# Hybrid retention, gated linear attention and sliding-window block: GLA queries and keys move into the paired products, branch products become the heads' filling, moving sums and stores in another order

## The chip, the cores and the metric

The kernel runs on one core of a Trainium2 chip. The time is device microseconds of one launch, the median over several runs. PE is the tensor engine, DVE the vector engine, ACT the scalar engine, POOL GpSimd, SP the sync engine, which here only issues DMAs.

## The reference

One transformer block on 1024 tokens of width 1024, in float32. All matmuls are wanted at nearly float32 accuracy.

```python
h = rmsnorm(x, norm_mix_pre)
proj = h @ w_in
rq, rk, rv, rg, gq, gk, gv, gg, ga, sq, sk, sv, gate_logits = split(proj)
o_ret = head_groupnorm(retention(rq, rk, rv)) * silu(rg)          # 4 heads, dk 128, dv 256
log_a = max(log_sigmoid(ga @ alpha2 + b) / 16, -1)
o_gla = head_rmsnorm(gla(gq, gk, gv, log_a)) * silu(gg)           # 4 heads, chunks of 64 tokens
o_swa = swa_sinks(sq, sk, sv, sinks)                              # 16 query heads, window 128
projected = einsum('bsnc,ncd->bsnd', stack(o_ret, o_gla, o_swa), w_branch)
merged = sum(sigmoid(gate_logits) * projected, over the 3 branches)
x = x + rmsnorm(merged @ w_out, norm_mix_post)
h = rmsnorm(x, norm_ffn_pre)
f = (silu(h @ w_gate) * (h @ w_up)) @ w_down                      # width 2816
x = x + rmsnorm(f, norm_ffn_post)
```

In GLA, queries are multiplied by exp(b) and keys by exp(-b), b the running sum of log_a within a chunk; these factors lie in DRAM as `ed`.

## The kernel before

Each float32 operand is cut into a rounded high part (a cast on ACT, line 127) and a residue (a subtraction on DVE, line 128); a product is three matmuls, high x high, high x low, low x high. So PE works in groups of three, mostly 128x128 weights on 512 moving columns (token halves).

The program goes through these stages. *First phase* (up to about 100 us): x is normed, transposed on PE in two token halves (tiles `xps`, `hf`, the halves `hT`), first products and the window's values (`swa_values`, tile `sv`) run between. *Dense products*: feature-major columns of w_in go through `class Pairs`: two column blocks by two token halves form a 2x2 block product that is done with seven block products in place of eight (Strassen-Winograd): 84 matmuls for two blocks. `p1` to `p7` are the seven; the stationary sums s1 to s4 are made by `sums`/`split` from the weights, the moving sums t1 to t4 by `class Sums` from the normed input, made once. `steps` runs the first `lead` pairs together, so that each t is made and used once for all, then the rest in turn; results leave as held outputs (`held`) and snapshots `sn` in SBUF. *Window attention*, with token-major values v as filling (`lin_values`). *Heads*: eight recurrences (four of retention, four GLA, `i` from 0 to 7); each has short products with waits between, and takes filling from `lin_fill`: a generator that gives 12 matmuls per step. *Branches* (`branches`): 24 products of w_branch, 48 matmuls each, times the gate, summed over the branches into `mgd`. *Output rows* (`out_mm`, `out_norm`, eight rows, stores x1d), *feed-forward up* (pairs of gate and up columns, again with `Pairs`, lead 3, stores fT), *down* (`down_load`, `down_mm`, two token halves, stores out).

The GLA queries and keys go through `lin_qk`: plain products, 48 matmuls per column block, in `lin_stream` behind each head's values, as filling of the heads. The first partial sums of the branches stay in SBUF.

Tiles come from pools: 45 slots of 4 KB per partition (`dt_`), 18 of 2 KB (`bt`), eight PSUM banks. In the first part (line 76) the instructions of an engine stand in the order in which the code is written; from there on a scheduler sets the order per engine from its estimates. The queues are in order: a DMA that waits for a slot holds all that stand behind it on the same engine.

## Time and profile before

| | |
|---|---|
| median of 3 runs | 2200.08 us (2199.95 to 2202.84) |
| profiled execution | 2200.43 us |
| its span, first to last instruction | 2198.7 us |
| mean granted clock of PE | 0.983 |
| PE, DVE, ACT, POOL busy | 96%, 55%, 42%, 11% |

A busy share is an average over all stages. A matmul is shown with its whole passage, so neighbours overlap; the time from one start to the next is what counts. "[6.00 <-ACT s L127]" means that the engine was idle for 6.00 us and that the instruction that ended this is the one of ACT on line 127 that wrote tile s.

### The profile page before, as it was taken

What the parts mean: (1) busy time and instruction counts of PE and PEld (TensorE: products, weight loads), DVE (VectorE), ACT (ScalarE), POOL (GpSimd) and SP (SyncE); (2) the same over time, 40 slices, a digit from 0 to 9 for tenths busy, and PEclk for the clock granted to TensorE, in tenths of its full rate; (3) what the DMA queues carried; (4) which work ended last, traced back from release to release, by engine and by line L of the source; (5) the groups of instructions that cost most, each with busy time, mean ns of one, the idle gap of its engine ahead of it and who ended that gap; (6) DMA issues with size and microseconds to landing.
All of it is one profiled execution on the core that took longest, in us unless ns stands there. A gap on an engine that the chain in (4) does not pass through costs nothing. (4 is left out here: it accounts for less than half of the span.)

```text
span 2198.7 us, 28731 instructions
## 1 busy us (share of the span) xinstructions
PE 2114.9 (96%) x10660; PEld 1789.7 (81%) x10660; DVE 1205.9 (55%) x2219; ACT 914.1 (42%) x1772; POOL 240.9 (11%) x413
## 2 busy tenths in 40 slices
PE   6899999999999999999989999998999999999998
PEld 5678888888889989998967888876788888878786
DVE  4778754444438986555554444346565555544351
ACT  5455544444447774444342221255433333343240
POOL 3011000000012322332321000031000000000000
PEclk8999999999999999999989999999999999999999
DMA  5369655555565437656474542242454455473441
GB/s 186 108 215 271 211 168 172 161 161 159 179 221 179 150 132 268 239 190 228 149 263 138 173 144 96 96 134 77 132 146 136 138 144 144 125 267 140 169 176 39
DMA packets 343277, 364.06 MB, mean 166 GB/s; under 512 B 16464, under 2 KB 267728, under 8 KB 343136
## 3 DMA queue, kind: packets, MB, share of 16 engines
q1 hardware_dynamic: 299776, 265.20, 39.4%
q10 hardware_dynamic: 30816, 54.02, 6.7%
q0 software_dynamic: 12544, 43.00, 5.1%
q8 instruction: 84, 1.38, 0.3%
q14 instruction: 57, 0.47, 0.1%
HBM read 264.64 MB, written 97.52 MB: 165 GB/s over the span
## 5 line engine op out<-in xcount | busy, mean ns | idle before, releaser
L128 DVE TENSOR_TENSOR wl<-raw,wh 128x1024 fp32r<-128x1024 f32 x131 | 159.9, 1221 | 149.0 <-ACT wh L127 83.4
L127 ACT CAST s<-raw 128x512 fp32r<-128x512 f32 x200 | 120.6, 620 | 225.1 <-DVE raw L381 73.5
L127 ACT CAST wh<-raw 128x1024 fp32r<-128x1024 f32 x141 | 147.2, 1046 | 149.7 <-DMA raw<-in_w_down 58.9
L406 PE MATMUL x<-t,s 128*128 128x512 f32 x408 | 158.2, 392 | 5.7 <-ACT s L127 2.8
L407 PE MATMUL x<-t,s 128*128 128x512 f32 x408 | 159.7, 391 | 0.5 <-DVE t L128 0.3
L408 PE MATMUL x<-t,s 128*128 128x512 f32 x408 | 159.1, 390 | 0.0
L242 PE MATMUL pf<-o,wh 128*128 128x512 f32 x384 | 148.8, 394 | 8.4 <-ACT o L127 8.4
L243 PE MATMUL pf<-o,wh 128*128 128x512 f32 x384 | 149.7, 392 | 0.2 <-DVE o L128 0.2
L257 PE MATMUL v<-wh,hT 128*128 128x256 f32 x512 | 146.2, 285 | 0.0
L356 ACT COPY sn<-x 128x512 f32<-128x512 f32 x151 | 88.2, 585 | 137.3 <-PE x L408 131.0
L259 PE MATMUL v<-wh,hT 128*128 128x256 f32 x512 | 145.2, 284 | 0.0
L258 PE MATMUL v<-wl,hT 128*128 128x256 f32 x512 | 145.2, 284 | 0.0
L1334 PE MATMUL dn<-wh,f 128*128 128x512 f32 x352 | 137.0, 392 | 4.2 <-ACT f L127 4.2
L1335 PE MATMUL dn<-wl,f 128*128 128x512 f32 x352 | 136.9, 391 | 0.0
L128 DVE TENSOR_TENSOR s<-raw,s 128x512 fp32r<-128x512 f32 x200 | 134.4, 686 | 2.2 <-ACT s L127 1.7
L245 PE MATMUL pf<-o,wl 128*128 128x512 f32 x384 | 121.2, 391 | 0.0
L1203 POOL TENSOR_TENSOR rr<-rr,mhalf 128x1 f32<-128x1 f32 x16 | 8.7, 541 | 961.7 <-DVE rr L1202 961.7
L1337 PE MATMUL dn<-wh,f 128*128 128x512 f32 x352 | 109.1, 390 | 0.0
L258 PEld LDWEIGHTS v<-wl,hT 128*128 128x128 f32 x512 | 98.4, 192 | 1.1
L257 PEld LDWEIGHTS v<-wh,hT 128*128 128x128 f32 x512 | 98.4, 192 | 1.1
L259 PEld LDWEIGHTS v<-wh,hT 128*128 128x128 f32 x512 | 98.4, 192 | 0.0
L406 PEld LDWEIGHTS x<-t,s 128*128 128x128 f32 x408 | 76.6, 188 | 23.4 <-ACT s L127 3.2
(304 smaller groups left out, 5374.2 us busy)
## 6 DMA issues: line engine op xcount, KB each, us to landing
raw<-in_w_in SPq DMA_DIRECT2D x138, 512.0 KB, 5.8
raw<-in_w_down SPq DMA_DIRECT2D x44, 512.0 KB, 7.0
raw<-in_w_gate SPq DMA_DIRECT2D x43, 512.0 KB, 4.2
raw<-in_w_up SPq DMA_DIRECT2D x43, 512.0 KB, 4.6
v<-v POOLq DMA_DIRECT2D x32, 512.0 KB, 3.9
v<-v SPq DMA_DIRECT2D x32, 512.0 KB, 6.7
gT<-go ACTq DMA_DIRECT2D x48, 256.0 KB, 3.4
raw<-in_w_branch SPq DMA_DIRECT2D x24, 512.0 KB, 5.7
```

The costliest lines, as they stand in the source:

```text
L127: se.copy(out=hi, in_=src)
L128: return (eng or ve).tensor_tensor(out=lo, in0=src, in1=hi, op=ALU.subtract)
L242: pe.matmul(p_, lhsT=wh, rhs=hi, start=(k == 0), stop=False)
L243: pe.matmul(p_, lhsT=wh, rhs=lo, start=False, stop=False)
L257: pe.matmul(ps, lhsT=lh, rhs=rh, start=start, stop=False)
L258: pe.matmul(ps, lhsT=lh, rhs=rl, start=False, stop=False)
L259: pe.matmul(ps, lhsT=ll, rhs=rh, start=False, stop=stop)
L406: pe.matmul(ps, lhsT=h, rhs=hi, start=(start and k == 0), stop=False, skip_group_check=True)
L407: pe.matmul(ps, lhsT=h, rhs=lo, start=False, stop=False, skip_group_check=True)
L408: pe.matmul(ps, lhsT=l, rhs=hi, start=False, stop=(k == KH - 1), skip_group_check=True)
L1334: pe.matmul(ps[ch], lhsT=fh[:, ts_], rhs=ws[ch][0], start=(first and i == 0), stop=False)
L1335: pe.matmul(ps[ch], lhsT=fh[:, ts_], rhs=ws[ch][1], start=False, stop=False)
```

## The change

Five things change. (1) The GLA queries and keys become four more keys ("qk", 1, h) of the pairs in the dense products; their outputs are multiplied by `ed`, which SP loads, and stored by ACT. `lin_qk` is gone. Matmuls of 128x512 go from 7388 to 7340, those of other shapes stay as they were. (2) All value products are through before head 4, and then `lin_fill` gives branch products; the first branch's gated product goes to DRAM (`mg0`) and comes back when the second is added. (3) In the first phase, both products of pair 1 and the second group of values stand before the transposes of the second token half. (4) t1 is written into dead storage together with t4's subtraction moved to a method of its own; t1 and s1 are made before the held outputs; the next pair's sums come earlier; weights of the feed-forward pairs are fetched and cut earlier. (5) The stores x1d, fT and out go from ACT's queue to POOL's.

```diff
@@ Pairs.steps
-                held.append(self.p2(n, True))
+                h = self.p2(n, i or lead < 3)
+                if h:
+                    held.append(h)
...
             self.products(first, [x[n] for n in first], "s2", "t2", False)
+            self.make("t1")
+            for n in first:
+                self.split(n, "s1")
             for h in held:
...
-            self.make("t1")
             for n in first:
-                self.split(n, "s1")
                 z[n] = bank("z")
...
                 self.p1(nxt)
+                self.sums(nxt)
...
                 self.p2(nxt)
-                self.sums(nxt)
@@ Sums
         def t1(self):
             res = []
             for k, (t3, t2) in enumerate(self.t):
-                b21, b22 = self.h[k + KH]
-                ve.tensor_tensor(out=b21, in0=b21, in1=t2, op=ALU.subtract)
-                ve.tensor_tensor(out=t2, in0=b22, in1=t2, op=ALU.subtract)
-                res.append(moving("t1", t2))
+                o = self.h[k][1]
+                ve.tensor_tensor(out=o, in0=self.h[k + KH][1], in1=t2, op=ALU.subtract)
+                pr = bpair("t1")
+                self.last = split(*pr, o)
+                res.append(pr)
+            return res
+
+        def t4(self):
+            res = []
+            for k, (t3, t2) in enumerate(self.t):
+                o = self.h[k + KH][0]
+                ve.tensor_tensor(out=o, in0=o, in1=t2, op=ALU.subtract)
+                res.append(moving("t4", o))
             return res
@@ keys of the dense products and their outputs
     ikeys += [("silu", br, c) for br in range(2) for c in range(0, NK, 2)]
+    ikeys += [("qk", 1, h) for h in range(H)]
...
         if kind == "qk":
...
+            if br:
+                e = bt("ed")
+                sp.dma_start(out=e, in_=ed[c][row][:, t])
+                ve.scalar_tensor_tensor(out=g, in0=src, scalar=1.0 if row else DK ** -0.5, in1=e,
+                                        op0=ALU.mult, op1=ALU.mult)
...
+            se.dma_start(out=qkd[br][c][row][:, t], in_=g)
@@ first phase
     swa_values(0)
+    inp.blocks(ikeys[1])
+    next(steps)
+    next(steps)
+    inp.sums(ikeys[0])
+    swa_values(2)
     for k in range(NK):
...
         if k == 3:
-            inp.blocks(ikeys[1])
-    inp.sums(ikeys[0])
-    swa_values(2)
-    next(steps)
-    next(steps)
-    inp.sums(ikeys[1])
+            inp.sums(ikeys[1])
@@ heads and branches
             yield from lin_values(H + h)
-            yield from lin_qk(h)
...
-        if bi == 0:
+        if bi == 1:
             mgd[c] = dt_("mgd")
+            sp.dma_start(out=mgd[c], in_=mg0[c])
...
+        if bi == 0:
+            po.dma_start(out=mg0[c], in_=gt)
...
-            while done[0] < 16 * (i + 2 - H):
-                lin_fill(1)
+            if i + 1 == H:
+                done[0] += len([0 for _ in stream])
+                xT.clear()
             nxt = lin_load(i + 1)
         else:
-            run(stream)
-            xT.clear()
@@ output rows, feed-forward, down
-        se.dma_start(out=x1d[t], in_=x1)
+        po.dma_start(out=x1d[t], in_=x1)
...
-        se.dma_start(out=fT[f][:, th * TH:(th + 1) * TH], in_=o)
+        po.dma_start(out=fT[f][:, th * TH:(th + 1) * TH], in_=o)
...
         if t == 5:
-            up.fetch(1)
+            up.fetch(2)
...
         if t == 7:
+            up.blocks(1)
             up.sums(0)
...
-    up.blocks(1)
     next(ups)
...
-                (sp if t == NT - 1 else se).dma_start(out=out[t * P:(t + 1) * P, cs], in_=o[ch])
+                (sp if t == NT - 1 else po).dma_start(out=out[t * P:(t + 1) * P, cs], in_=o[ch])
```

How the order moves: PE in the first phase, before. sv are the window's values, xps the transposes, x and y the first two products of pair 1.

```order
L76 MATMUL sv_400<-wh_395,hT_340 128x272
L76 MATMUL xps_457<-ident,xn_311 128x128
...
L76 MATMUL xps_467<-ident,xn_311 128x128
...
L76 MATMUL xps_531<-ident,xn_311 128x128
...
L76 MATMUL sv_551<-wh_387,hT_293 128x272
...
L76 MATMUL x_609<-hT_293,wh_497 128x512 x2
...
L76 MATMUL y_624<-hT_325,wh_497 128x512 x2
...
L76 MATMUL sv_671<-wh_387,hT_464 128x272
```
The same place after:

```order
L76 MATMUL sv_400<-wh_395,hT_340 128x272
L76 MATMUL x_461<-hT_293,wh_457 128x512 x2
...
L76 MATMUL y_476<-hT_325,wh_457 128x512 x2
...
L76 MATMUL sv_499<-wh_387,hT_293 128x272
...
L76 MATMUL xps_557<-ident,xn_311 128x128
...
L76 MATMUL xps_567<-ident,xn_311 128x128
...
L76 MATMUL xps_637<-ident,xn_311 128x128
...
L76 MATMUL sv_671<-wh_387,hT_564 128x272
```
x, y and one group of values stand ahead of the transposes now; the next values (sv_671) keep their place behind.

DVE, the moving sums of one k in the first phase, before (line 569 is t4's subtraction; t1's, line 570, follows later):

```order
L76 TENSOR_TENSOR t_114_647<-hf_506,hf_462 128x512
L76 TENSOR_TENSOR t_114_647<-t_114_647,hf_291 128x512
L569 TENSOR_TENSOR hf_323<-hf_323,t_114_647 128x512
L76 TENSOR_TENSOR t_115_650<-t_114_647,t_115_650 128x512
```
After (line 571 is t1's subtraction, 581 t4's):

```order
L76 TENSOR_TENSOR t_114_647<-hf_612,hf_562 128x512
L76 TENSOR_TENSOR t_114_647<-t_114_647,hf_291 128x512
L571 TENSOR_TENSOR hf_562<-hf_612,t_114_647 128x512
L581 TENSOR_TENSOR hf_323<-hf_323,t_114_647 128x512
L76 TENSOR_TENSOR t_115_650<-t_114_647,t_115_650 128x512
```
Both subtractions stand at the first sum now.

PE at the end of head 6 before. o, us, q are the recurrence, kt and ap the next head's scores, pf the branch products.

```order
L257 MATMUL o_11118<-us_11130,q_10853 128x256
...
L942 MATMUL kt_11166<-ident,kf_10985 128x128 x4
L957 MATMUL ap_11174<-qf_10984,kf_10985 128x64
...
L942 MATMUL kt_11193<-ident,kf_10985 128x128 x4
...
L957 MATMUL ap_11201<-qf_10984,kf_10985 64x64
L242 MATMUL pf_11287<-o_11219,wh_10702 128x512
...
L242 MATMUL pf_11288<-o_11222,wh_10702 128x512
```
After, at the end of head 3, where the branch products begin:

```order
L1001 MATMUL yt_10223<-ident,y_9720 128x128 x4
...
L256 MATMUL kv_10257<-v_9711,n_10112 128x256
...
L256 MATMUL o_10258<-v_9711,a_10122 128x256
...
L256 MATMUL o_10258<-us_10267,q_10104 128x256
...
L241 MATMUL pf_10347<-o_10273,wh_9823 128x512
...
L241 MATMUL pf_10348<-o_10276,wh_9823 128x512
...
L244 MATMUL pf_10347<-o_10273,wl_9824 128x512
```
Before, the first branch product stands behind the last scores with nothing of the head around it; now it stands among the products kv and o of a head.

ACT at the start of the feed-forward, before. t are casts of the moving sums, s of the stationary ones, sn snapshots of PSUM, fo the silu of held outputs.

```order
L127 CAST t_2330_14161<-t_2329_14158 128x512
...
L127 CAST t_2336_14179<-t_2335_14176 128x512
L356 COPY sn_14227<-x_14014 128x512
L1268 ACT_TABLE_LOAD
L1268 ACTIVATE fo_14218<-fo_14218 128x512
...
L127 CAST t_2345_14239<-t_2329_14158 128x512
...
L127 CAST s_2349_14257<-raw_13736 128x512
...
L127 CAST s_2353_14265<-raw_14011 128x512
L127 CAST t_2355_14305<-t_2329_14158 128x512
```
After:

```order
L127 CAST t_2379_14268<-t_2378_14265 128x512
...
L127 CAST t_2385_14286<-t_2384_14283 128x512
L127 CAST t_2386_14326<-h2f_13964 128x512
...
L127 CAST t_2389_14338<-h2f_13967 128x512
L127 CAST s_2390_14341<-raw_13840 128x512
...
L127 CAST s_2392_14347<-raw_14115 128x512
L355 COPY sn_14356<-x_14118 128x512
...
L127 CAST a22h_14469<-raw_13840 128x512
L1273 ACTIVATE fo_14350<-fo_14350 128x512
...
L127 CAST t_2403_14405<-t_2378_14265 128x512
```
The casts of t1 (t_2386 and on) and s1 (s_2390 and on) stand directly behind t2's, the snapshots and silus behind them.

ACT at the step to the second token half of the down products before, with the stores in its queue:

```order
L1200 ACTIVATE o_17835,ms_2874_17837<-dn_17124 128x512
L1200 ACTIVATE o_17836,ms_2874_17837<-dn_17125 128x512
L1200 ACTIVATE o_17863,ms_2879_17865<-dn_17138 128x512
L1200 ACTIVATE o_17864,ms_2879_17865<-dn_17139 128x512
L1368 DMA out<-o_17835 128x512
L1368 DMA out<-o_17836 128x512
L1200 ACTIVATE o_17891,ms_2884_17893<-dn_17152 128x512
```
After, POOL has them between the powers of the norm (line 1208):

```order
L1282 DMA fT_13347<-fo_17068 128x512 x2
L1208 TENSOR_TENSOR rr_17944<-rr_17944,mhalf 128x1
L1372 DMA out<-o_17939 128x512
L1372 DMA out<-o_17940 128x512
L1208 TENSOR_TENSOR rr_17972<-rr_17972,mhalf 128x1
L1372 DMA out<-o_17967 128x512
```
The stores are in POOL's queue now, and the next row's power stands behind two of them.

## Rows read from the trace of the kernel before

**Rows 1.** the page, busy time, share of the span and instructions of each engine

```profile
PE 2114.9 (96%) x10660; PEld 1789.7 (81%) x10660; DVE 1205.9 (55%) x2219; ACT 914.1 (42%) x1772; POOL 240.9 (11%) x413
```

**Rows 2.** by stretch: length; busy PE, PEld, DVE, ACT, POOL; clock, DMA share, GB/s

```profile
385.00:440.00 55.00, 55.00 (x245) 45.53 (x244) 25.43 (x37) 26.93 (x41) 0.00 (x0) 1.00 0.54 163
1100.00:1155.00 55.00, 44.58 (x240) 36.66 (x239) 32.62 (x70) 23.23 (x46) 15.92 (x24) 0.88 0.73 263
1485.00:1540.00 55.00, 43.48 (x189) 33.41 (x187) 38.48 (x63) 30.53 (x70) 6.41 (x11) 0.92 0.25 77
```

**Rows 3.** what PE waited for: total us, times, longest

```profile
PE z L406 <- ACT s L127: 12.3, 2, 6.3
PE pf L242 <- ACT o L127: 8.4, 1, 8.4
...
PE dn L1334 <- ACT f L127: 4.2, 2, 3.9
PE x L406 <- ACT wh L127: 3.8, 1, 3.8
```

**Rows 4.** PE in time, first phase: start, us, instruction, [idle before]

```profile
42.34 3.22 PE L76 MATMUL xps<-ident,xn 128*128 128x128 f32 x28
...
88.82 0.80 PE L406 MATMUL z<-t,s 128*128 128x512 f32 x1 [6.00 <-ACT s L127]
...
96.93 0.39 PE L406 MATMUL x<-t,s 128*128 128x512 f32 x1
```

**Rows 5.** DVE in time, first phase

```profile
44.35 0.69 DVE L76 TENSOR_TENSOR hT<-hf,hT 128x512 fp32r<-128x512 f32 x1 [0.87 <-ACT hT L76]
...
47.63 0.69 DVE L76 TENSOR_TENSOR hT<-hf,hT 128x512 fp32r<-128x512 f32 x1 [0.55 <-ACT hT L76]
...
57.77 0.68 DVE L76 TENSOR_TENSOR raw<-raw,raw 128x512 f32<-128x512 f32 x1
...
63.89 0.68 DVE L76 TENSOR_TENSOR raw<-raw,raw 128x512 f32<-128x512 f32 x1
...
69.18 0.68 DVE L76 TENSOR_TENSOR t<-hf,hf 128x512 f32<-128x512 f32 x1
...
86.74 2.49 DVE L128 TENSOR_TENSOR t<-t,t 128x512 fp32r<-128x512 f32 x4
```

**Rows 6.** PE in time, head 6

```profile
1110.69 2.46 PE L957 MATMUL ap<-qf,kf 128*128 128x64 f32 x16
1121.60 0.79 PE L242 MATMUL pf<-o,wh 128*128 128x512 f32 x1 [8.44 <-ACT o L127]
...
1128.29 0.47 PE L243 MATMUL pf<-o,wh 128*128 128x512 f32 x1
```

**Rows 7.** PE in time, start of the feed-forward

```profile
1507.84 0.79 PE L406 MATMUL x<-b,wh 128*128 128x512 f32 x1 [3.76 <-ACT wh L127]
...
1523.73 0.96 PE L406 MATMUL x<-t,s 128*128 128x512 f32 x3 [0.43 <-ACT t L127]
...
1540.17 0.79 PE L406 MATMUL z<-t,s 128*128 128x512 f32 x1 [6.28 <-ACT s L127]
...
1575.33 0.79 PE L406 MATMUL x<-t,s 128*128 128x512 f32 x1 [2.76 <-ACT s L127]
```

**Rows 8.** ACT in time, ahead of the wait that ends at 1540.17

```profile
1537.42 2.18 ACT L127 CAST t<-t 128x512 fp32r<-128x512 f32 x4
1539.50 1.66 ACT L127 CAST s<-raw 128x512 fp32r<-128x512 f32 x3
```

**Rows 9.** DVE in time, the last output row

```profile
1507.84 0.75 DVE L1233 TENSOR_SCALAR xn<-x,rstd 128x1024 f32<-128x1024 f32 x1 [2.54 <-POOL rstd L141]
```

**Rows 10.** POOL in time, a DMA issue

```profile
666.19 0.57 POOL L925 DMA_DIRECT2D v<-v  x1 [3.80 <-PE so L869]
```

**Rows 11.** ACT in time, a DMA issue

```profile
1432.18 0.33 ACTq L1228 DMA_DIRECT2D x<-x  x1
```

**Rows 12.** SP in time, loads at the second token half

```profile
2023.75 40.21 SPq L1326 DMA_DIRECT2D rf<-fT  x4
```

More of the change, by code (lines that the diff above doesn't have):

```diff
@@ L200, in block_kernel @@
     plan = [("tm", "in", RV + h * DV) for h in range(H)]
-    for h in range(H):
-        plan += [("tm", "in", GV + h * DV), ("fm", "in", GQ + h * DK), ("fm", "in", GK + h * DK)]
+    plan += [("tm", "in", GV + h * DV) for h in range(H)]
     plan += [("fm", ("br", br), c * P) for br in branch_order for c in range(NK)]
@@ L577, in all @@
         def all(self):
-            return {"t2": self.t2, "t1": self.t1, "t3": self.t3, "t4": self.block(range(KH, NK), 0)}
+            return {"t2": self.t2, "t1": self.t1, "t3": self.t3, "t4": self.t4}
     gate_in, gates_gla = {}, []
@@ L658, in in_load @@
         if kind == "qk":
-            c0 = RQ + c * DK, RK + c * DK
+            c0 = (RQ, GQ)[br] + c * DK, (RK, GK)[br] + c * DK
         else:
@@ L689, in in_out @@
         if kind == "qk":
-            mul = decay[row][:, c * P:(c + 1) * P].unsqueeze(1).broadcast_to([P, 4, P])
-            ve.tensor_tensor(out=chunked(g), in0=chunked(src), in1=mul, op=ALU.mult)
-            se.dma_start(out=qkd[0][c][row][:, t], in_=g)
+            if br:
[3 more added lines that the diff above has]
+                                        op0=ALU.mult, op1=ALU.mult)
+            else:
+                mul = decay[row][:, c * P:(c + 1) * P].unsqueeze(1).broadcast_to([P, 4, P])
+                ve.tensor_tensor(out=chunked(g), in0=chunked(src), in1=mul, op=ALU.mult)
+            se.dma_start(out=qkd[br][c][row][:, t], in_=g)
             return
@@ L896, in lin_load @@
         return st
-    def lin_qk(h):
-        def done(z):
-            def store(ps):
-                for th in range(2):
-                    t = slice(th * TH, (th + 1) * TH)
-                    o = bt("qk")
-                    sp.dma_start(out=o, in_=ed[h][z][:, t])
-                    ve.scalar_tensor_tensor(out=o, in0=ps[th], scalar=1.0 if z else DK ** -0.5, in1=o,
-                                            op0=ALU.mult, op1=ALU.mult)
-                    po.dma_start(out=qkd[1][h][z][:, t], in_=o)
-            return store
-        yield from proj_steps(("fm", "in", GQ + h * DK), xT, done(0))
-        yield from proj_steps(("fm", "in", GK + h * DK), xT, done(1))
     def lin_values(i):
@@ L1119, in block_kernel @@
     mgd = [None] * NK
+    mg0 = [dram.tile([P, S], F32, name=f"mg0_{c}") for c in range(NK)]
     ms_ = [[None, None] for _ in range(NK)]
@@ L1130, in branch_evac @@
         gts = halves(gt)
-        if bi == 0:
+        if bi == 1:
             mgd[c] = dt_("mgd")
+            sp.dma_start(out=mgd[c], in_=mg0[c])
         for th in range(2):
-            dst = mgd[c][:, th * TH:(th + 1) * TH]
             if bi == 0:
-                ve.tensor_tensor(out=dst, in0=ps[th], in1=gts[th], op=ALU.mult)
+                ve.tensor_tensor(out=gts[th], in0=ps[th], in1=gts[th], op=ALU.mult)
             else:
+                dst = mgd[c][:, th * TH:(th + 1) * TH]
                 ve.tensor_tensor(out=gts[th], in0=ps[th], in1=gts[th], op=ALU.mult)
                 ve.tensor_tensor(out=dst, in0=dst, in1=gts[th], op=ALU.add)
+        if bi == 0:
+            po.dma_start(out=mg0[c], in_=gt)
     def branches():
@@ L1301, in block_kernel @@
             up.blocks(0)
-            up.fetch(2)
             out_transpose(4, xns.pop(4))
         if t == 7:
+            up.blocks(1)
             up.sums(0)
```

## The prediction

> **What bounds the kernel now.** I began with the busy times of the page: TensorE (PE) works for 96% of the span, the next engine, VectorE (DVE), for 55% [rows 1]. So a microsecond can be won in two ways only: less work on PE, or fewer holes in it. The table by stretches says where the holes are. In the dense stretch from 385 us PE is busy for all of its 55 us with 244 weight loads, at clock 1.00: one 128x512 product every 55 / 244 = 0.2254 us. The stretches from 1100 and from 1485 us have 10.4 and 11.5 us idle, at clocks 0.88 and 0.92 [rows 2]. The list of PE's waits names the holes: z waits 12.3 us in two pieces, pf 8.4 us in one, dn 4.2, x 3.8 [rows 3]. These places are the first sums at 88.82 us, head 6 of the recurrences at 1121.60, the start of the feed-forward products (1507.84, 1540.17, 1575.33) and the step to the second token half of the down products (the dn wait) [rows 3, 4, 6, 7].
>
> A hole costs more than its idle time. After the 6.00 us wait, 24 z products run from 88.82 to 96.93 us, 8.11 us, where 24 x 0.2254 = 5.41 would do [rows 4]: 2.70 us more, because the granted clock is at its lower level at first (1.2 of 2.4 GHz; a z shows 0.80 us) and rises later. I use 2.7 as the price of a restart everywhere below.
>
> **Gated queries and keys as pairs.** Eight column blocks at 48 products go (384); four pairs at 84 come (336). PE has 48 fewer 128x512 products: 48 x 0.2254 = **-10.8 us**. Nothing hides it, since both versions run where PE is the bound. The edit's other work (a pair's sums on DVE, casts on ACT, loads of ed on SP, stores) lies beside a PE that is full: in the stretch from 385 us, which is made of such pairs alone, DVE has 25.4 and ACT 26.9 of 55 us [rows 2]. I cost it at 0. Its bound is one restart per pair, 4 x 2.7 = 10.8 us, if ed comes late each time; a pair takes PE 84 x 0.2254 = 18.9 us, of which the loads, in the same order as the weights, have most.
>
> **Filling of the heads.** Before, the filling of heads 0 to 5 uses up all the value and key products, and head 6 runs bare: after its last scores (1110.69, 2.46 long) PE stands 8.44 us for o, then stays at the lower clock until about 1128.3, where products are at 0.47 and below [rows 6]. With the 10.4 us idle of that stretch [rows 2] and half of the 6.7 us at the lower clock, 3.3, the bare head costs 13.7 us. After, all values are through at head 3 and the branch products fill from there on. The wait for the first o (its load, cast and residue) is not gone: it moves to head 3. But there the load is issued while GV values are still running, and the cast stands right behind the last state update of ACT; PE has its own kv and o products beside it. I put it at 1 us of idle and a restart of 2.7, so 3.7 of 13.7 come back: **-10 us**, between -13.7 (it is covered) and -4 (the wait comes back at full length with a part of the time at the lower clock).
>
> Heads 4 to 7 now have the branch's tiles live beside their own: eight o pairs, weights, a gate tile and, new, the store and reload of the first partial sums. Loads on SP wait there for free slots. No row shows this load in this place; the nearest is the last bare head. I take **+3 us** (one restart), between 0 and 14 (one more bare head).
>
> **The first phase.** Products x and y of pair 1 (24) and the second value group (48 of 128x272) now go ahead of the 32 transposes of the second token half, which stood at 42.34 us [rows 4]. That is no filling for a waiting PE alone: DVE is what paces this stretch. It makes one pair of transposed blocks in 3.28 us (44.35 to 47.63), so four in 13.1; it reaches the pair sums at 57.77 and the moving sums t at 69.18; the residues of t that z waits for run at 86.74 [rows 5]. With the new order the transposes can start only when PE is through: 24 x 0.2254 + 48 x 0.125 (an estimate, 0.2254 x 272/512, rounded up) = 11.4 us, plus the wait for the cast of the pair's weights and one restart, some 57 instead of 42.3, so 14.7 later. In that time DVE can do only the sums of pair 0 with the values' residues, 6.1 us (57.77 to 63.89), and the weight's residue, 1.2: it stands some 7. Back come up to 2.4, since t1 and s1 are cut ahead of the held outputs (four residues of 0.62, the 2.49 of [rows 5]). Net **+4 us** (7 less 2.4, rounded down as the transposes then also have fewer values between them), between -3 (the 6.00 us wait halves) and +8 (DVE stands for longer).
>
> **Start of the feed-forward.** Four waits stand there: 3.76 (weights' cast), 0.43, 6.28 (s behind the casts of t), 2.76 [rows 7]. The 6.28 has its reason in [rows 8]: ACT casts the four t1 at 1537.42 and the three s1 only at 1539.50, since the subtractions for t1 and the work on the three held outputs stood ahead. After, t1 and s1 are cut directly behind t2, the held outputs later; the blocks of pair 1 are made during the last output rows, and the next pair's sums one product earlier. Removed: 3.76 + 6.28 + 2.76 = 12.8 and three restarts, 8.1. But then PE reaches the t2 products sooner than DVE the sums t. PE would be there at 1523.73 - 0.43 - 3.76 - 2.7 = 1516.8. The last row's xn ends at 1508.6 on DVE [rows 9] as before; behind it stand the last transposes and four copies (1.1 each on PE and DVE), then in the new order a weight's residue (1.2), nine sums and residues of pairs, and t's own two, eleven at 0.6 each, then t's cast and residue (0.6 each): 1508.6 + 2.2 + 1.2 + 6.6 + 1.2 = 1519.8. So some 3.0 us of wait, about 1 us before the last transposes and one restart come back, 6.7. 20.9 - 6.7 = 14.2; I take **-13 us**, since the subtractions for t4 and the silus now crowd behind, between -6 (only the 6.28 goes) and -18.
>
> **Stores on POOL.** An issue holds POOL 0.57 us and ACT 0.33 [rows 10, 11]. For fT (44) and x1d (8) nothing waits behind them that PE needs within microseconds: cost 0, a gain of 0.33 per row on ACT that is off the chain. At the step to the second token half, POOL also raises the norm's power for the next row: that is queued behind two issues, and who waits for it is the row's scaling on DVE and with it the slots of the outputs. SP stands there for 40.21 us (four loads from 2023.75) [rows 12] for slots that these stores free, and PE then waits 3.9 in the longest dn wait [rows 3]. One more f block is loaded ahead in the new order of SP, 24 products or 5.4 us, more than the 3.9. **-2 us**, between -6.6 (wait and restart gone) and +4.6 (four rows of 2 x 0.57 in full, with the wait as it stands).
>
> The Trainium skill ("DMA: Bandwidth & Descriptors", section SWDGE vs HWDGE vs iDMA) says that DMAs issued from GpSimd get their descriptors from software, with a first byte at about 1 us against 0.6: it speaks against this edit. The trace agrees on the issue, 0.57 against 0.33 [rows 10, 11]. By the rule each store lands 0.4 us later, which changes the sum only at the second half, by 0.4 x 4 = 1.6 us, an estimate.
>
> **Sum.** -10.8 - 10 + 3 + 4 - 13 - 2 = -28.8 us. The profiled execution took 2200.43 us (span 2198.7 and 1.7 around it), 0.35 above the median of the runs: 2200.43 - 28.8 = 2171.6, less 0.35: 2171.
>
> **Rivals.**
> First: only the products are saved, and every hole moves: what the feed-forward start wins (-6) the first phase (+4) and the heads (+3) take back. 2200.1 - 10.8 = 2189 us. For it: DVE paces two of the places, and its work there does not shrink. Against: head 6 gets filling that it has not had at all.
> Second: the holes close and the first phase is neutral: -10.8 - 13.7 - 18 - 6.6 = -49.1, so 2151 us. For it: the names that the waits list are exactly those whose producers move forward. Against: DVE's 3.28 us cadence, which stays.
> Third, on the other side: filling that comes too late. Each branch product needs o, its weights and the gate tile, all through SP, whose order is fixed; if at heads 4 to 7 a load waits for a slot that only the head itself frees, PE stands bare at each of them: 4 x 13.7 = 55 us in place of the -10 and the +3. 2171 + 7 + 55 = 2233 us. It decides from between two and three such heads (28.8 / 13.7 = 2.1 with the gain at head 6 gone). For it: SP already stands 40 us in one piece elsewhere [rows 12]. Against: heads take their filling in steps of 12 products, 2.7 us, so a late tile delays one step, and PE has the head's own products meanwhile.
> Fourth: the early products do not fill a hole at all (the edit doesn't do what its name says), which is the +4 at its upper end, +8: it is in the range.
>
> **How the numbers follow.** Forecast 0.69; first rival 0.15, second 0.08, third 0.06, others 0.02. The forecast's own range takes the terms' distances to their bounds as independent (root of the sum of squares): upwards 6, 11, 4, 7 and 6.6 give 16; downwards 3.7, 3, 7, 5 and 4.6 give 11: 2160 to 2187. It is widened to 2190, to hold the first rival, and to 2154, to hold what comes near the second; the third stays outside. A measurement of this kernel tells 0.2% (4.4 us) from no change. Faster by more than that: 0.69 + 0.15 + 0.08 - 0.01 = 0.91; within: 0.03; slower: 0.06.
>
> **What would show it.** In the profile of the changed kernel: 48 products fewer on PE, and the dense stretch still full; no 8.4 us wait of pf before head 4's end, and the stretch of head 6 full at clock 1.00; the first z later than 88.82 by some 4 us; at the feed-forward start one wait ahead of x<-t of some 3.6 us and none over 1 us ahead of z. It is wrong if PE waits for o, wh or a gate tile at several heads, if the first z starts before 86 or after 97, or if the 6.28 us wait merely changes its name.

## The result and the profile after

The changed kernel takes 2174.61 us (2173.23 to 2176.93, 4 runs) against 2200.8 us before (4 runs by then): ratio 0.9881, 95% interval 0.9864 to 0.9898. The forecast was 2171 us, in a range of 2154 to 2190. The profiled execution has a span of 2172.0 us, 26.7 less than before.

The busy times of the page, against [rows 1]:

```profile
PE 2099.9 (97%) x10612; PEld 1777.2 (82%) x10612; DVE 1232.9 (57%) x2263; ACT 921.7 (42%) x1798; POOL 273.5 (13%) x471
```

PE has 48 matmuls fewer (10660 to 10612) and fills 97% of its span. The stretches, with the columns of [rows 2] (length; busy PE, PEld, DVE, ACT, POOL; clock, DMA share, GB/s):

```profile
385.00:440.00 55.00, 55.00 (x245) 45.53 (x244) 29.27 (x42) 19.88 (x34) 0.00 (x0) 1.00 0.58 177
1045.00:1100.00 55.00, 52.34 (x273) 43.37 (x274) 36.98 (x72) 28.23 (x50) 14.59 (x25) 0.97 0.76 254
1155.00:1210.00 55.00, 52.35 (x290) 43.29 (x289) 31.56 (x66) 26.55 (x51) 14.33 (x30) 1.00 0.73 258
1210.00:1265.00 55.00, 52.09 (x264) 42.77 (x265) 37.22 (x77) 15.40 (x30) 13.69 (x22) 0.97 0.61 196
1485.00:1540.00 55.00, 48.97 (x209) 38.32 (x208) 43.95 (x72) 32.45 (x68) 5.22 (x9) 0.94 0.16 51
```

The dense stretch is as full as before, with DVE at 29.3 us in place of 25.4. No stretch of the heads has 10 us idle any more; but now three of them have 2.7 to 2.9 each. The start of the feed-forward is idle for 6.0 us in place of 11.5. What PE waited for (total, times, longest), against [rows 3]:

```profile
PE z L627 <- DVE g L614: 5.7, 1, 5.7
PE o L256 <- ACT us L1045: 4.8, 5, 1.8
PE h2t L1250 <- DVE xn L1238: 4.6, 1, 4.6
...
PE pf L241 <- ACT o L127: 2.0, 2, 1.3
```

The four names of [rows 3] are gone or small: z for s 0.6 in place of 12.3, pf for o 2.0 in place of 8.4, no dn and no 3.8 us wait for wh in the feed-forward. In their place stand z for g (3.5 before), o for us and h2t for xn.

A sum over all of PE's rows shows where the time went. For each matmul I took the time to the next one's start, less what it needs at the full pitch (0.2254 us for 512 columns, 0.1188 for 256, 0.1251 for 272, 0.099 for 128, 0.05 for 64; the same for all kernels, so only differences count). What is left is PE's loss, waits and lower clock together, in us. The stages: up to the first z; to 12 us past the first gate product z<-g; to 3 us ahead of the first window score ss; to the first kt; to the last yt; to the first pr; to the first dn; to the end.

| kernel (profiled span) | to first z | to 12 us past the first gate product | dense | window attention | heads | branches | output rows, feed-forward | down |
|---|---|---|---|---|---|---|---|---|
| before (2198.7) | 34.6 | 9.7 | 5.3 | 16.7 | 39.9 | 1.3 | 32.1 | 7.9 |
| changed (2172.0) | 36.3 | 12.1 | 6.0 | 16.5 | 40.1 | 0.7 | 17.7 | 1.3 |
| first phase in old order (2165.4) | 30.1 | 11.9 | 5.9 | 16.7 | 40.1 | 0.7 | 17.6 | 1.3 |
| alpha2 early (2164.0) | 37.1 | 2.9 | 6.5 | 16.7 | 39.8 | 0.7 | 17.7 | 1.3 |
| norm later (2166.6) | 37.5 | 11.5 | 6.2 | 15.2 | 35.8 | 0.7 | 17.4 | 1.3 |
| held outputs first (2187.7) | 43.4 | 13.9 | 6.3 | 16.6 | 39.9 | 0.7 | 24.4 | 1.3 |
| heads without filling (2208.5) | 36.2 | 12.3 | 6.4 | 16.7 | 74.1 | 2.5 | 17.5 | 1.3 |
| out stores on ACT (2176.2) | 36.2 | 12.2 | 5.9 | 16.5 | 40.1 | 0.7 | 17.8 | 5.9 |
| first sums in SBUF (2176.1) | 37.8 | 11.4 | 6.0 | 16.5 | 41.2 | 0.7 | 19.4 | 1.3 |
| plain queries and keys (2187.5) | 38.1 | 12.1 | 5.8 | 17.1 | 42.0 | 0.7 | 17.7 | 1.3 |
| three edits (2154.3) | 30.1 | 4.4 | 6.5 | 16.8 | 35.9 | 0.7 | 17.3 | 1.3 |
| norm at the head's end (2151.2) | 29.9 | 3.0 | 6.4 | 14.9 | 36.2 | 0.7 | 17.7 | 1.3 |
| norm on POOL (2155.6) | 31.4 | 4.6 | 6.1 | 15.5 | 37.8 | 0.7 | 17.2 | 1.3 |
| norm on POOL and ACT (2150.2) | 30.1 | 3.0 | 7.3 | 16.7 | 32.5 | 0.7 | 17.4 | 1.4 |

Each row of the table is one execution. The seven kernels in which nothing of the changed first phase was undone lie between 36.2 and 38.1 in the first column, the five with the old order between 29.9 and 31.4: a difference under 2 us there says nothing. In the heads' column the five kernels whose heads nothing touched lie between 39.8 and 40.1. The expectations below quote losses of the heads that are up to 1.3 us lower (39.2, 34.6): in that sum some matmuls at the edges of a view were counted twice.

From before to the changed kernel: -10.8 for the products, +1.7 and +2.4 in the first phase, -0.1 in dense, window attention and branches together, +0.2 in the heads, -14.4 at the output rows and the feed-forward, -6.6 in down, and 1.0 more ahead of the first matmul's start and behind the last one's: -26.6, where the spans differ by 26.7. So the forecast's total is nearly met, but one term gave nothing: the heads.

The same sum by head (a head ends with the last of its transposes yt; 0 to 3 are retention, 4 to 7 GLA):

| kernel | 0 | 1 | 2 | 3 | 4 | 5 | 6 | 7 |
|---|---|---|---|---|---|---|---|---|
| before | 1.3 | 1.5 | 1.8 | 4.3 | 4.5 | 4.1 | 18.9 | 3.6 |
| changed | 2.2 | 0.8 | 1.8 | 11.3 | 4.0 | 6.0 | 8.4 | 5.6 |
| norm later | 2.2 | 0.8 | 1.2 | 11.4 | 4.0 | 4.8 | 7.4 | 4.1 |
| heads without filling | 2.2 | 0.8 | 1.8 | 14.0 | 12.9 | 13.4 | 12.8 | 16.2 |
| norm on POOL | 2.2 | 0.8 | 1.8 | 11.2 | 4.0 | 4.1 | 10.6 | 3.1 |
| norm on POOL and ACT | 2.2 | 0.8 | 1.8 | 11.3 | 4.0 | 4.0 | 6.4 | 2.0 |

Head 6 loses 10.5 us less than before. Head 3, where the branch products now begin, loses 7.0 more, and heads 5 and 7 together 3.9 more; that is the whole of what head 6 won.

The heads, PE in time, against [rows 6]:

```profile
1047.18 0.50 PE L241 MATMUL pf<-o,wh 128*128 128x512 f32 x1 [1.33 <-ACT o L127]
...
1160.18 0.39 PE L256 MATMUL o<-us,q 128*128 128x256 f32 x1 [1.04 <-ACT us L1045]
...
1201.60 0.38 PE L256 MATMUL o<-us,q 128*128 128x256 f32 x1 [1.23 <-ACT us L1045]
...
1251.63 0.39 PE L256 MATMUL o<-us,q 128*128 128x256 f32 x1 [1.80 <-ACT us L1045]
```

The 8.44 us wait for the branch's o is down to 1.33, at head 3. Around it, though, stand waits of 0.83 (for DVE's tu), 0.34 and 0.68, and from 1045 to 1066 us the granted clock is 0.92: 7.4 of head 3's 11.3 us are lost between 1042 and 1066. In heads 5 to 7 three waits for the state's cast us are new. In the 6 us from 1160 and from 1201 us the granted clock stays at 1.00, in those from 1251, at the longest of the three, it is 0.72. ACT ahead of the second of them, and POOL's row that releases it:

```profile
1195.45 0.51 ACT L1045 ACTIVATE us<-tu,mid 128x256 fp32r<-128x256 f32 x1 [1.36 <-DVE tu L1041]
...
1199.44 1.70 ACT L992 ACTIVATE y<-y,rstd 128x256 f32<-128x256 f32 x4 [3.49 <-POOL rstd L141]
1201.05 0.49 ACT L1045 ACTIVATE us<-tu,mid 128x256 fp32r<-128x256 f32 x1
```

```profile
1198.37 1.04 POOL L141 TENSOR_TENSOR rstd<-rstd,mhalf 128x4 f32<-128x4 f32 x1
```

ACT stands 3.49 us for the norm's rstd, multiplies y for 1.70 us, and only then casts the state (us, 0.49), whose input DVE had written by 1197.77. PE waits for that cast until 1201.60.

The first phase, PE in time, against [rows 4]:

```profile
43.74 0.73 PE L76 MATMUL x<-hT,wh 128*128 128x512 f32 x2 [1.41 <-ACT wh L76]
...
59.55 0.66 PE L76 MATMUL xps<-ident,xn 128*128 128x128 f32 x4 [0.95 <-DVE hf L76]
...
68.15 0.59 PE L76 MATMUL sv<-wh,hT 128*128 128x272 f32 x1 [4.20 <-ACT hf L76]
...
90.86 0.50 PE L405 MATMUL z<-t,s 128*128 128x512 f32 x1 [0.63 <-ACT s L127]
...
137.38 0.77 PE L627 MATMUL z<-g,a 96*128 96x512 f32 x1 [5.73 <-DVE g L614]
```

The products x of pair 1 now fill PE from 43.74, the transposes stretch to 63 us with waits for DVE, the next values wait 4.20 us for the first block of the second half. The first z comes at 90.86 with a wait of 0.63 in place of 6.00. Then z for g, the first product of the GLA gates, waits 5.73 (3.5 before). Its chain begins on SP:

```profile
102.74 26.97 SPq L541 DMA_DIRECT2D raw<-in_w_in  x8
129.76 1.70 SPq L599 DMA_DIRECT2D al<-in_alpha  x1
```

```profile
135.04 0.62 ACT L602 CAST a<-al 16x512 fp32r<-16x512 f32 x1 [4.39 <-DMA al<-in_alpha]
```

The small load of alpha2 (al) stands behind eight weight loads, which wait for slots until 129.71; ACT gets it at 135.04.

The feed-forward, PE in time, against [rows 7]:

```profile
1503.10 0.90 PE L1250 MATMUL h2t<-ident,xn 128*128 128x128 f32 x3 [4.57 <-DVE xn L1238]
...
1516.11 0.98 PE L405 MATMUL x<-t,s 128*128 128x512 f32 x3 [0.96 <-ACT t L127]
...
1526.12 0.44 PE L405 MATMUL z<-t,s 128*128 128x512 f32 x1
```

One wait of 4.57 for the last row's xn, one of 0.96 ahead of the t2 products, and none ahead of z (before: 3.76, 0.43, 6.28, 2.76). From the last eight transposes to 60 us behind the first z the loss is 11.4 in place of 23.8; 2.1 more are saved in the output rows ahead of them.

### The profile page after: what moved, and what is told of

It reads as the page before. It is cut to its first block, busy times and chain, and to the rows that moved or that the text cites. A ratio compares the mean times of both kernels' runs of the same rounds, so it can differ in the third digit from the quotient of the medians.

```text
span 2172.0 us, 28893 instructions
## 1 busy us (share of the span) xinstructions
PE 2099.9 (97%) x10612; PEld 1777.2 (82%) x10612; DVE 1232.9 (57%) x2263; ACT 921.7 (42%) x1798; POOL 273.5 (13%) x471
## 5 line engine op out<-in xcount | busy, mean ns | idle before, releaser
L128 DVE TENSOR_TENSOR wl<-raw,wh 128x1024 fp32r<-128x1024 f32 x127 | 155.2, 1222 | 146.9 <-ACT wh L127 75.9
L127 ACT CAST s<-raw 128x512 fp32r<-128x512 f32 x216 | 130.2, 621 | 209.6 <-DVE raw L380 91.3
L406 PE MATMUL x<-t,s 128*128 128x512 f32 x440 | 171.7, 390 | 0.5 <-DVE t L128 0.3
L407 PE MATMUL x<-t,s 128*128 128x512 f32 x440 | 171.3, 389 | 0.0
L405 PE MATMUL x<-t,s 128*128 128x512 f32 x440 | 170.0, 390 | 1.2 <-ACT t L127 1.0
L355 ACT COPY sn<-x 128x512 f32<-128x512 f32 x163 | 95.1, 586 | 139.5 <-PE x L407 115.4
L128 DVE TENSOR_TENSOR s<-raw,s 128x512 fp32r<-128x512 f32 x216 | 145.4, 687 | 3.1 <-ACT s L127 2.5
L406 PEld LDWEIGHTS x<-t,s 128*128 128x128 f32 x440 | 82.6, 188 | 19.3 <-DVE t L128 2.2
L405 PEld LDWEIGHTS x<-t,s 128*128 128x128 f32 x440 | 82.5, 188 | 19.2 <-ACT t L127 1.4
```

Of the source, the lines that this page charges most:

```text
L127: se.copy(out=hi, in_=src)
L128: return (eng or ve).tensor_tensor(out=lo, in0=src, in1=hi, op=ALU.subtract)
L405: pe.matmul(ps, lhsT=h, rhs=hi, start=(start and k == 0), stop=False, skip_group_check=True)
L406: pe.matmul(ps, lhsT=h, rhs=lo, start=False, stop=False, skip_group_check=True)
L407: pe.matmul(ps, lhsT=l, rhs=hi, start=False, stop=(k == KH - 1), skip_group_check=True)
```

## Experiments

All are edits of the changed kernel; none leaves work out. The held outputs, the heads without filling, the stores on ACT, the first sums in SBUF and the plain queries and keys were run once, the others four or five times. With one execution an effect is read from the table above, stage by stage, rather than from the time.

**First phase in the old order.**

```diff
     swa_values(0)
-    inp.blocks(ikeys[1])
-    next(steps)
-    next(steps)
-    inp.sums(ikeys[0])
-    swa_values(2)
     for k in range(NK):
```

(and they stand behind the transposes again)

> The changed kernel with the first phase in the old order (transposes of the second token half ahead of the products of pair 1 and of the second group of values); all else as changed. In the changed kernel the loss of PE against its full pitch up to 160 us is 56.2 us, before it was 51.6. Theory (DVE paces the stretch, the early products only push the transposes back): the old order gives 2 to 4 us back, the first z starts near 88 us, with a wait of a few us ahead of it, total about 2171 where the changed kernel has 2174.6. Rival (the order is neutral, and the 4.5 us come from the later load of alpha's weights alone): the first z stays at 90 to 91 and the time within 1 us of the changed kernel.

2170.12 us, ratio to before 0.9858 (0.9841 to 0.9874). PE in time:

```profile
84.51 0.50 PE L405 MATMUL z<-t,s 128*128 128x512 f32 x1 [1.20 <-ACT s L127]
...
131.04 0.77 PE L627 MATMUL z<-g,a 96*128 96x512 f32 x1 [5.72 <-DVE g L614]
```

The first z comes 6.3 us sooner, its stage loses 6.2 us less, and the gate's wait stays at 5.72. The theory holds against its rival, with more than its 2 to 4 us: 4.5 between the medians, 6.6 between the profiled executions, of which this one is the fastest of its four runs. With t1 and s1 made early, the early products cost some 6 us.

**alpha2 loaded ahead of the weights.**

```diff
-        al = bt("al")
-        sp.dma_start(out=al[:RANK, :], in_=alpha2)
+        al = gate_in.pop("al")
...
+        if i == 1:
+            gate_in["al"] = bt("al")
+            sp.dma_start(out=gate_in["al"][:RANK, :], in_=alpha2)
         if i == 8:
```

> The changed kernel with one load moved: the 16x512 weights of the GLA gate (alpha2, tile al), which stand on SP behind eight weight loads that wait for slots, are issued ahead of them. PE's wait z <- g is 5.7 us there (3.5 before), and the matmuls behind it run at the lower clock. Theory (the load's place in SP's queue makes that wait): the wait goes, 5.7 us and some 2.7 of restart, 8 us less, about 2166.5. Rival (the transposes of ga and the copies on DVE are as late): the wait keeps 2 us or more, and under 4 us are won.

2165.55 us, ratio 0.9832 (0.9817 to 0.9846). No wait for g over 0.5 us is left; the gate's stage loses 2.9 in place of 12.1. The load's place in SP's queue was the cause, worth 9.2 us in that stage, 8.0 in the span and 9.1 between the medians. The wait was there before the change too, with 3.5 us.

**Norm of the first four chunks one pair later.**

```diff
-            if c0 == 2:
+            if c0 == 4:
                 lin_norm(br, ys[0])
```

> The changed kernel with the norm of each head's first four chunks written one pair of chunks later. In the changed kernel the heads lose as much of PE as before (39 us), although the 8.4 us wait of head 6 is gone: PE waits for o <- us at 1160, 1202 and 1252 us (1.0, 1.2, 1.8 us, each with a restart), where ACT stood 3.5 to 5.4 us for the norm's rstd from POOL with the state's cast us queued behind it. Theory (that queue on ACT is what the waits come from): they go or shrink under 0.5 us at two of the three places, 5 to 9 us less, about 2167. Rival (POOL or the state's chain itself is late): o <- us waits stay at the same total, time within 2 us of 2174.6.

2170.77 us, ratio 0.9855 (0.9841 to 0.987): 3.8 us less between the medians, between the theory's 5 to 9 and the rival's 2. The heads lose 4.3 us less (the table by head: 1.2, 1.0 and 1.5 of it in heads 5 to 7). Of the three waits (1.04, 1.23, 1.80) the first is gone, two remain, and one of them is not smaller:

```profile
1196.98 0.39 PE L256 MATMUL o<-us,q 128*128 128x256 f32 x1 [1.38 <-ACT us L1045]
...
1249.88 0.39 PE L256 MATMUL o<-us,q 128*128 128x256 f32 x1 [0.95 <-ACT us L1045]
```

So this run moves the waits and does not settle their cause: the scheduler put another state cast behind the later norm.

**Held outputs ahead of t1 and s1.**

```diff
-            self.make("t1")
-            for n in first:
-                self.split(n, "s1")
             for h in held:
```

(and the three lines stand behind the held outputs again)

> The changed kernel with one part undone: t1 and s1 are made behind the held outputs again, in the dense products and in the feed-forward. Theory (the 6.28 us wait of before at the feed-forward start came from the casts of t1 and s1 behind the silus and outputs): z waits about 5 to 7 us again there, and 3 to 6 us at the first sums, each with a restart of 2.7: 9 to 17 us more, 2184 to 2191. Rival (the earlier weights and sums of the next pairs did it): under 4 us more.

2189.48 us, span 15.7 longer. PE's waits ahead of z, and ACT ahead of the second:

```profile
97.97 0.80 PE L405 MATMUL z<-t,s 128*128 128x512 f32 x1 [5.91 <-ACT s L127]
...
1539.37 0.79 PE L405 MATMUL z<-t,s 128*128 128x512 f32 x1 [4.34 <-ACT s L127]
```

```profile
1534.61 1.15 ACT L1272 ACTIVATE fo<-fo 128x512 f32<-128x512 f32 x2
...
1536.60 2.19 ACT L127 CAST t<-h2f 128x512 fp32r<-128x512 f32 x4
1538.68 1.67 ACT L127 CAST s<-raw 128x512 fp32r<-128x512 f32 x3
```

As in [rows 8], the casts of t and s come behind snapshots and silus. 7.1 and 1.8 us more loss in the first phase and 6.7 at the feed-forward: the theory's size, near its upper end, though the wait at the feed-forward (4.34) is under the 5 to 7 expected. With the rest of the change in place, these three lines are worth 15.7 us of the span.

**Heads without filling.**

```diff
-            elif not xT:
+            elif not xT and done[0] < 0:
                 next(branch_fill, None)
```

> The changed kernel with the filling taken from heads 3 to 7: once the values are through, the heads get no branch products; these follow in one piece behind head 7. Same work in all. Theory (a bare head costs what head 6 cost before, 13.7 us, and the filled heads of the changed kernel still lose some 3 us each): 4 heads more by 10 to 14 us each, 40 to 55 us more, 2215 to 2230. Rival (the heads' own chain is so short that the filling is worth little): under 20 us more.

2210.26 us, span 36.5 longer, between theory and rival. The heads lose 34.0 us more: 2.7 at head 3 and 4.4 to 10.6 at each of the four GLA heads. PE's largest waits are for y, at every head from 3 on:

```profile
1067.19 0.96 PE L1001 MATMUL yt<-ident,y 128*128 128x128 f32 x3 [6.33 <-ACT y L990]
...
1091.66 0.69 PE L1001 MATMUL yt<-ident,y 128*128 128x128 f32 x2 [5.11 <-ACT y L992]
```

A bare GLA head loses 12.8 to 16.2 us, as the 13.7 said; a filled one in the changed kernel still loses 4.0 to 8.4. So the filling is worth the difference, 7.8 us a head on average, not 10 to 14.

**Stores of out on ACT.**

```diff
-                (sp if t == NT - 1 else po).dma_start(out=out
+                (sp if t == NT - 1 else se).dma_start(out=out
```

> The changed kernel with the stores of out on ACT again; SP's order is the same. In the changed kernel the 3.9 us wait of dn at the second token half is gone (5.4 us of PE loss before, 0 now). Theory (the third f block, loaded ahead in SP's new order, covers it; the stores' queue does not matter): still no dn wait over 0.5 us there, time within 1.5 us of 2174.6. Rival (the stores on POOL free the slots earlier): the wait returns with 3 to 4 us and its restart, 5 to 6.6 us more.

2178.03 us, span 4.2 longer. The wait is back, with 2.62 us:

```profile
2057.90 1.14 PE L1338 MATMUL dn<-wh,f 128*128 128x512 f32 x3 [2.62 <-ACT f L127]
```

ACT ahead of it in this kernel:

```profile
2045.16 0.62 ACT L127 CAST f<-rf 128x512 fp32r<-128x512 f32 x1 [2.06 <-DVE rr L1207]
...
2056.28 1.04 ACT L127 CAST wh<-raw 128x1024 fp32r<-128x1024 f32 x1 [6.16 <-DMA raw<-in_w_down]
2057.23 0.61 ACT L127 CAST f<-rf 128x512 fp32r<-128x512 f32 x1
```

In the changed kernel, ACT:

```profile
2042.60 0.62 ACT L127 CAST f<-rf 128x512 fp32r<-128x512 f32 x1
```

The cast that PE waits for stands behind a cast of weights that come late by DMA. SP, in this kernel:

```profile
2001.71 38.93 SPq L1330 DMA_DIRECT2D rf<-fT  x4
```

and in the changed one:

```profile
1998.15 3.48 SPq L1330 DMA_DIRECT2D rf<-fT  x4
...
2003.54 3.53 SPq L1330 DMA_DIRECT2D rf<-fT  x4
...
2012.17 29.11 SPq L1330 DMA_DIRECT2D rf<-fT  x4
```

What these loads waited for (total, times, longest), with the stores on ACT and then in the changed kernel:

```profile
SPq L1330 <- DMA out<-o: 40.8, 6, 35.0
```

```profile
SPq L1330 <- DMA out<-o: 40.4, 7, 27.0
```

The rival holds: the queue of the stores decides when loads of the second half find slots. The order of these loads is the same, but with the stores on ACT the third load of an rf (a part of fT) waits 35.0 us for a store of out to finish, and SP stands as in [rows 12]. In the changed kernel ten loads of rf are issued before SP comes to such a wait, which is 27.0 us long. So the loads ahead that cover the wait come with the move of the stores. Why rf gets other slots is not shown. The stores also hold ACT itself: the first f is cast 2.56 us later, behind issues of stores that wait for DVE's sums. The run does not part the two. Together they are 4.6 us of loss in down, of the 6.6 that the changed kernel saved; the remaining 2.0 were not taken apart.

**First branch sums in SBUF.**

```diff
-        if bi == 1:
+        if bi == 0:
             mgd[c] = dt_("mgd")
-            sp.dma_start(out=mgd[c], in_=mg0[c])
...
-        if bi == 0:
-            po.dma_start(out=mg0[c], in_=gt)
```

> The changed kernel with the first branch's gated products kept in SBUF as before, with no store and reload. Theory (the heads' remaining waits come from the norm in ACT's queue, not from the round trip): the o <- us waits stay (1.0, 1.2, 1.8 us), time within 2 us of 2174.6. Rival (the eight stores of 0.57 us on POOL, ahead of the state's scaling, and the reloads in SP's queue make them): the waits fall by half or more, 4 to 8 us less. A third outcome, slots too few for eight more tiles, would show as new DMA waits in heads 4 to 7.

2178.18 us, 4.1 us more span. The heads lose 41.2, no less than with the round trip (40.1), so the rival falls. The waits did change places, against the theory's letter (one of 1.53 for y is new too):

```profile
1198.58 0.39 PE L256 MATMUL o<-v,a 128*128 128x256 f32 x1 [1.00 <-DVE tu L1041]
```

The 4.1 us are spread: 1.5 to the first z, where equal kernels differ as much, 1.1 in the heads, 1.7 at the output rows and feed-forward. I have no cause for them.

**Queries and keys as plain products.**

```diff
-    ikeys += [("qk", 1, h) for h in range(H)]
...
             yield from lin_values(H + h)
+            yield from lin_qk(h)
```

> The changed kernel with one part undone: GLA queries and keys as plain products again (48 matmuls per column block, behind each head's values, all through before head 4), the branch filling as changed. PE has 48 more 128x512 matmuls. Theory (pure PE work at 0.2254 us each): 10.8 us more, 2183 to 2188, nothing else moves by more than 2 us. Rival (the pairs cost something else, in DVE's sums or in late loads of ed): under 6 us more; or over 15 more, if heads 0 to 3 with twice the filling lose or win.

2189.24 us, span 15.5 longer. 10.8 are the 48 matmuls; 4.1 of loss are spread, 1.8 to the first z and 1.9 in the heads the largest parts. That is a little over the theory's range and at the edge of the rival's 15 us. The first of the two lies in what equal kernels differ by there; of the heads' 1.9, head 3 loses 3.6 more and the others win, without a cause that was shown.

**Three edits together** (first phase in old order, alpha2 early, norm one pair later).

> The changed kernel with three edits together: the old order of the first phase, alpha2 loaded ahead of the eight weights, the norm of a head's first four chunks one pair later. Alone they took 6.6, 8.0 and 5.4 us off the profiled span of 2172.0 us. Theory (they are three separate holes of PE): the sum, 20 us, span about 2152, time 2153 to 2156, ratio to before about 0.978. Rival (the holes share a cause or the schedules of the heads change again): under 15 us.

2156.04 us (2152.51 to 2159.13), ratio 0.9794 (0.9779 to 0.9808); the span is 17.7 us shorter, of 20 expected, and the median 18.6, where the three alone add up to 17.4. They are separate holes.

**The same with both norms behind the head's last chunk.**

```diff
-            if c0 == 4:
-                lin_norm(br, ys[0])
+        lin_norm(br, ys[0])
         lin_norm(br, ys[1])
```

> As the combined kernel, but with both norms of a head behind its last chunk. Theory (what the heads lose is the state's cast us behind the norm on ACT): no o <- us wait over 0.3 us in heads 4 to 7 and 2 to 4 us less than the combined kernel. Rival (the heads' outputs come so late that the next wait takes the place, for the transposes yt or for the branch's o): within 2 us of the combined kernel, or more.

2154.26 us, ratio 0.9789 (0.9776 to 0.9803), not to be told from the kernel above. The theory's 2 to 4 us are not met; the size is the rival's, but not its cause. Waits of 1.37 and 0.95 us for us remain, since the scheduler puts a state cast behind the norm again; ACT:

```profile
1178.54 0.91 ACT L994 ACTIVATE y<-y,rstd 128x256 f32<-128x256 f32 x2 [2.33 <-POOL rstd L141]
...
1179.35 0.49 ACT L1047 ACTIVATE us<-tu,mid 128x256 fp32r<-128x256 f32 x1
```

**GLA norm on POOL, state scaling on DVE** (with the old first phase and the early alpha2).

```diff
-                se.activation(out=yj[j], in_=yj[j], func=AF.Copy, scale=r[:, j:j + 1])
+                po.tensor_scalar(out=yj[j], in0=yj[j], scalar1=r[:, j:j + 1], scalar2=None, op0=ALU.mult)
...
-                        po.tensor_scalar(out=u, in0=tmp, scalar1=to_mid(c), scalar2=to_end(c + 1),
+                        (ve if br else po).tensor_scalar(out=u, in0=tmp, scalar1=to_mid(c), scalar2=to_end(c + 1),
```

> The old order of the first phase and the early alpha2 as in the combined kernel, the norm written at its old place, but for GLA its multiplication done on POOL in place of ACT, and the state's scaling tu for GLA on DVE in place of POOL. So in heads 4 to 7 nothing on ACT waits for the norm's rstd. Theory (the o <- us waits are the state's cast queued behind that wait): no o <- us wait over 0.4 us in heads 4 to 7, heads' loss of PE about 30 us against 34.6 in the combined kernel and 39.2 in the changed one, 3 to 6 us less than the combined kernel's 2156. Rival (DVE, with one scaling more per chunk, or the late y make a new wait): within 2 us of the combined kernel or slower.

2157.33 us, ratio 0.9803 (0.9787 to 0.9819): no faster than the three edits, as the rival said. But all waits for ACT's us over 0.3 us in heads 4 to 7 are gone, which is what the theory said of their cause, and heads 5 and 7 lose 1.9 and 2.5 us less than in the changed kernel; the price is at head 6, where the late y make a new wait. PE and POOL:

```profile
1210.53 0.44 PE L1003 MATMUL yt<-ident,y 128*128 128x128 f32 x2 [2.20 <-POOL y L994]
```

```profile
1206.89 6.66 POOL L994 TENSOR_SCALAR y<-y,rstd 128x256 f32<-128x256 f32 x4
```

**The same, the norm of a head's last four chunks on ACT.**

```diff
+                if first:
                     po.tensor_scalar(out=yj[j], in0=yj[j], scalar1=r[:, j:j + 1], scalar2=None, op0=ALU.mult)
+                else:
+                    se.activation(out=yj[j], in_=yj[j], func=AF.Copy, scale=r[:, j:j + 1])
```

> As the kernel with the GLA norm's multiplication on POOL, but only for a head's first four chunks; for the last four it is on ACT again. That kernel had no o <- us wait over 0.3 us left in heads 4 to 7, yet waited 2.2, 1.5 and 0.5 us for yt at 1210 us, where POOL took 6.66 us for the last four chunks' multiplication. Theory (those three waits were the price, the queue on ACT the cause): no o <- us and no yt wait over 0.6 us, 4 to 6 us less of span than the 2155.6 there, so about 2150, time 2151 to 2153. Rival (the scheduler's new order gives another wait of the same size): within 2 us of 2155.6.

2152.39 us (2151.62 to 2155.35), ratio 0.9781 (0.9766 to 0.9795); span 2150.2, as expected. The heads lose 32.5 in place of 40.1, and what is left of the waits for y and us is small: 0.32 us for y, and for us

```profile
1181.34 0.39 PE L257 MATMUL o<-us,q 128*128 128x256 f32 x1 [0.54 <-DVE us L1051]
```

This is the best version by its median: 22 us under the changed kernel, 48 under the one before. Its interval overlaps that of the two kernels with the norm moved; only the heads' column tells them apart (32.5 against 35.9 and 36.2). Two things moved at once here, the norm's multiplication and the state's scaling; neither was run alone.

## Why the prediction was right, and where not

The total is met to 3.6 us, in part by luck: the heads gave 7.2 us less than forecast, the stores and the feed-forward 6.0 more.

- **Products, -10.8.** Right: 48 matmuls gone, the dense stretch still full, its loss 0.7 us more. With the edit undone the last matmul comes 14.9 us later, 10.8 and 4.1 of loss elsewhere. The term's upper bound (10.8 more) was left out of the root that gives the range; with it the upper end is 2191.
- **Heads, -10 + 3.** Wrong: +0.2. The step that failed is the -10, in both of its parts. The 3.7 that were to come back at head 3 were 7.0: the wait for the first o is short (1.33), but others stand beside it and the clock is at 0.92 until 1066. No run took that place apart; in every run with filled heads but the one with plain queries and keys (14.9) head 3 loses 11.2 to 11.4. And 13.7 at head 6 was 10.5: a bare head does lose that much (12.8 to 16.2 in the run without filling), but I set the filled one at nothing, and it loses 8.4. The +3 for heads 4 to 7 has the right size (3.4 in heads 4, 5 and 7) by another cause: I looked for late loads on SP, and it was a queue on ACT, where the norm's multiplication, waiting for POOL's rstd, stands ahead of the state's cast. With that multiplication off ACT for the first four chunks, and the state's scaling on DVE, heads 5 to 7 lose 7.6 us less. The third rival, filling that comes late through SP, did not happen. The stretch of head 6 is not quite full, as I had said it would be: from 1180 to 1227 us PE is idle for 2.2 of 47, at clock 1.00.
- **First phase, +4.** The size is right (+1.7 and +2.4), the account only in part. Up to the first z two effects nearly cancel: the early products cost 8.8 us with t1 and s1 behind the held outputs and 6.2 with them ahead, where I had 7; making t1 and s1 ahead gave 7.1 in the new order and 4.5 in the old, where I had 2.4 (8.8 and 4.5 are against the kernel before, so with the rest of the change in them). The +2.4 behind it is the gate's weights, which I had not looked at: a load behind eight others on SP. The sum is right by luck.
- **Start of the feed-forward, -13.** Right: -12.4 there, and -2.1 in the output rows. The waits that I placed are there in the other order: 4.57 ahead of the last transposes, where I had 1, and 0.96 ahead of the t2 products, where I had 3.0. Undoing the order of t1 and s1 gives 6.7 back, so about half of the gain is that edit's; the rest was not taken apart.
- **Stores on POOL, -2.** The size was off: -6.6, the lower bound. The cover that I named, loads ahead, is there, but more of it than one block, and it comes with the stores' move: on ACT again, SP stands 38.93 us in place of the 40.21 of before, and 4.6 us come back. The Trainium skill (DMA: Bandwidth & Descriptors, section SWDGE vs HWDGE vs iDMA, the times of the first byte in its section Latency and other measured facts) spoke against this edit, by up to 1.6 us, an estimate. The trace agrees in direction: the issue is longer (1.14 us for two on POOL, 0.94 on ACT), and a store of out lands 2.6 us after its issue (median), where it took 2.1 with the stores on ACT again and 2.4 before. The move gained even so: what counts here is what waits for the store, and what stands behind it in its queue.

## What to carry to other kernels

In an in-order queue, look behind every instruction that waits: here a cast of 0.5 us behind a multiplication that waits 3.5 for another engine stopped PE, and a 32 KB load behind eight loads that wait for slots cost 9 us. When a large hole is filled, count the same loss again in the neighbouring stages before booking the gain: what the filled head 6 saved, head 3, to which the start of the branch products moved, and two GLA heads lost. And a bare stretch's loss is an upper bound for what filling saves: take off what filled stretches of the same kind lose.

## What the runs showed of the hardware

Some short POOL operations stretch beside DVE's residues. In the changed kernel POOL's scaling tu takes 0.56 us at 1149.88, and 1.39 at 1151.92, while DVE runs a residue of 128x1024 from 1151.66:

```profile
1149.88 0.56 POOL L1050 TENSOR_SCALAR tu<-tu,mid,end 128x256 f32<-128x256 f32 x1 [0.84 <-DVE tu L1041]
...
1151.92 1.39 POOL L1050 TENSOR_SCALAR tu<-tu,mid,end 128x256 f32<-128x256 f32 x1 [1.48 <-DVE tu L1041]
```

```profile
1151.66 1.22 DVE L128 TENSOR_TENSOR wl<-raw,wh 128x1024 fp32r<-128x1024 f32 x1
```

All seven POOL scalings of this shape in the changed kernel that take over 1.3 us lie beside a residue for about 1 us or more; the other 57 take 0.92 or less, among them three that lie beside a residue for 0.5 us and still take 0.55 to 0.56. With the norm on POOL four of its multiplications took between 3.65 and 6.66 us. That the residues are the cause is argued from such coincidences, not tested.
